# Keeping TensorE's source order in two stretches of a diffusion block's first mixer

## The chip, the cores and the metric

The kernel runs on one core of a Trainium2 chip. The metric is device time in microseconds (us), from launch to end, as a median of runs. The engines that matter here are TensorE (PE, matmuls and their weight loads), VectorE (DVE), ScalarE (ACT), GpSimd (POOL) and the queue of SyncE (SP), which issues most of the transfers. Each engine runs its own list of instructions in order; between engines they wait for each other through semaphores.

## The reference, cut to what matters

Two layers, each a mixer and a mixture of experts. The change touches the first mixer (`even_mixer`), which works on 256 context and 512 latent tokens, 768 in all:

```python
def even_mixer(a_lat, a_ctx, w_in, w_out, ...):
    cq_l, ckv_l, kr_l, rq_l, rk_l, rv_l, rg_l = split_cols(a_lat @ w_in, EVEN_SPLITS)
    ...                                   # the same for the context
    att_l = dense_block_attention(q_l, concat([k_c, k_l]), concat([v_c, v_l]))
    ret_l, ret_c = bidirectional_retention(...)
    y_lat = concat([att_l, retention_output(ret_l, rg_l, ret_norm_g)]) @ w_out

def modulation(cvec, w, b):               # six vectors of 1024 for each layer
    m = jax.nn.silu(cvec) @ w + b

def retention_output(o, g, gn_g):         # mean and variance over each head's 128 values
    y = head_layernorm(o, RET_GN_EPS).reshape(...) * gn_g
    return jax.nn.silu(g) * y
```

Attention has 8 heads of 64 + 32 (softmax over 256 keys for context rows and 768 for latent rows), retention has 4 heads of 128.

## The kernel before, in words

The program is written with a tile framework: pools hand out buffers in turn, semaphores come from the data, and a scheduler may reorder the instructions of each engine when the program is built. It lists them in the order in which they become ready in its own model of the machine. Inside `with tc.manual_schedule(engines={...PE})` the instructions of TensorE keep the order of the source; the other engines are still ordered by the scheduler. The experts' stage already runs inside such a block (L1695 to L2071), the first mixer does not.

The first mixer has two stretches that the change touches.

**Projections (L415 to L535).** `low_rank()` and `ret_proj()` are generators that make 20 column blocks of the input projection. Each block loads 128 columns of the weights (`load_w`: transfer `wraw`, then a high part by ACT, L401, and a low part by POOL, L402) and, after a `yield`, multiplies them with the activations in `proj_T`: for each half of the tokens (n = 0, 1) 8 row blocks k, and for each k three matmuls (L411 to L413), of `ah[k]`, `al[k]` and `ah[k]` again. `ah` and `al` are the high and low parts of the normalized activations, made just before by ACT (L380) and DVE (L382), one k after the other. At each `yield` two steps of the generator `ada` run: the modulation of both layers (`ada_gen`, L231), 40 chunks of 1 MB in all, each followed by 4 matmuls of 128x32 by 128x512 (8 records in the trace). Its ring holds 3 chunks, so the transfer of a chunk waits for the matmuls of the third before it.

**Attention beside retention (L556 to L704).** Two generators take turns, one step each. `mla()` runs 4 pairs of heads (hp) by 6 row tiles (t): `scores` (the matmuls `sc` into one of two double banks; row maximum L596 and its scaling L597 on DVE, exponential with row sum L599 on ACT, reciprocal L600 and multiplication of the row L601 on DVE, for head a = 0 and then a = 1, which I call P0 and P1 when done), a yield, then `values` of the tile before (matmuls `po`, L625) and `turn` of this one (transposes `ptp`, L615, of P0 and then P1, copied by ACT, L617). The step t = 0, 1 is narrow (256 keys: 2 `ptp` for a head, 4 `po`), t = 2 to 5 is wide (768 keys: 6 `ptp` for a head, 12 `po`); `values` belongs to the tile before, so the wide step t = 2 still has the 4 `po` of t = 1. Between t = 5 of a pair and its `turn` stands `heads` of the next pair (28 matmuls). `ret()` runs 4 heads by 6 tiles: the matmuls `rs` (L661, L671) and their masking on DVE (`sm`, L665, L674), a yield, then `rot` of the tile before (L694) and the matmuls `ro` (L682), whose statistics go through DVE (L686 to L688), a power on POOL (L689) and the normalization on DVE (`on`, L690). All banks other than those of `sc` come from one ring of four.

Because `heads` takes a step of its own, the two generators shift against each other by one step with each pair: for pairs 0 and 2 a step runs `sc`, `rot`, `ro`, `po`, `ptp`, `rs`; for pairs 1 and 3 it runs `rot`, `ro`, `sc`, `rs`, `po`, `ptp`.

Of the kernel before, what the change touches and what calls it, by code (L numbers as in the profile page):

```python
# [99 lines left out]
class Kern:  # L100
# [203 lines left out]
    def mixer0(self):  # L304
        nc, io, tc = self.nc, self.io, self.tc
# [24 lines left out]
        ada = self.ada_gen(0, 0)  # L330
# [53 lines left out]
        def ada_rest():  # L384
            for l, s in ((0, 1), (0, 2), (1, 0), (1, 1), (1, 2)):
                yield from self.ada_gen(l, s)
        ada = ada_rest()

        def load_w(cols, m=128):

            n = 32 if m == 64 else m
            raw = wsp.tile([128, 8, 128], F32, name="wraw")
            w = wsp.tile([128, 2, 8, 128], F32R, name="wblk")
            nc.sync.dma_start(raw[:, :, 0:n], wsrc[:, :, cols:cols + n])
            if m == 64:

                for b in range(2):
                    nc.vector.tensor_copy(
                        raw[:, :, 32:64].rearrange("p k (a b c) -> p k a b c", a=2, b=2)[:, :, :, b],
                        raw[:, :, 0:32].rearrange("p k (a b c) -> p k a b c", a=2, b=2)[:, :, :, 1 - b])  # L400
            nc.scalar.activation(w[:, 0, :, 0:m], raw[:, :, 0:m], AF.Copy)  # L401
            nc.gpsimd.tensor_tensor(w[:, 1, :, 0:m], raw[:, :, 0:m], w[:, 0, :, 0:m].bitcast(F32), OP.subtract)  # L402
            return w
# [21 lines left out]
        def low_rank():  # L425
            sqs = []
            for i in range(3):
                w = load_w(128 * i)
                dst = cqT[:, i] if i < 2 else ckvT
                sqt = new("sqt")  # L430
                sqs.append(sqt)

                def cb(n, t, p):
                    nc.scalar.activation(sqt[:, t], p, AF.Square)
                    nc.vector.tensor_copy(dst[:, t], p)
                yield
                proj_T(w, cb)
            nc.sync.dma_start(cs, io["k_cs"])
            nc.sync.dma_start(rcos, io["k_rcos"])
            nc.sync.dma_start(rsin, io["k_rsin"])  # L440
            w = load_w(384, 64)
            krt = new("krt")


            def cbk(n, t, p):
                nc.vector.tensor_tensor(krt[64:96, t], p[0:32], cs[64:96, t], OP.mult)
                nc.vector.tensor_tensor(kr[64:96, t], p[32:64], cs[96:128, t], OP.mult)
                nc.vector.tensor_tensor(kr[64:96, t], kr[64:96, t], krt[64:96, t], OP.add)
            yield
            proj_T(w, cbk, 64)  # L450
            nc.gpsimd.tensor_copy(kr[96:128], kr[64:96])
            for which in range(2):
                parts = sqs[0:2] if which == 0 else sqs[2:3]
                width = 256 if which == 0 else 128
                pbs = []
                for n in range(2):
                    pb = self.bank("ssb")
                    pbs.append(pb)
                    for i, s in enumerate(parts):
                        nc.tensor.matmul(pb[:, :384], self.ones, s[:, 384 * n:384 * n + 384], start=i == 0,  # L460
                                         stop=i == len(parts) - 1)
                rstd = new("rstd")
                for n, pb in enumerate(pbs):
                    r = rstd[:, 384 * n:384 * n + 384]
                    nc.vector.tensor_scalar(r, pb[:, :384], 1.0 / width, EPS, OP.mult, OP.add)
                    nc.scalar.activation(r, r, AF.Sqrt)
                    nc.vector.reciprocal(r, r)
                if which == 0:
                    for i in range(2):
                        nc.vector.scalar_tensor_tensor(cqT[:, i], cqT[:, i], self.qng[:, i:i + 1], rstd, OP.mult, OP.mult)  # L470
                else:
                    nc.vector.scalar_tensor_tensor(ckvT, ckvT, self.kvg, rstd, OP.mult, OP.mult)
# [54 lines left out]
        def ahead():  # L527
            yield from ret_proj()
            first.append(load(0))
        for gen in (low_rank(), ahead()):  # L530
            for _ in gen:
                next(ada, None)
                next(ada, None)
        for _ in ada:
            pass  # L535
        st_a.close()


# [111 lines left out]
        def ret():  # L650

            last = None
            for h in range(4):
                mk = bw.tile([128, 1536], F32, name="mk", bufs=1)
                nc.sync.dma_start(mk, io["k_masks"][h])
                for t in range(6):
                    ks_ = range(1, -1, -1) if t < 2 else range(5, 1, -1)
                    sm = bw.tile([128, 6, 128], F32, name="sm")
                    pb = self.bank("rs")
                    for i, kt in enumerate(ks_):  # L660
                        nc.tensor.matmul(pb[:, 128 * i:128 * i + 128], rk[h][:, 128 * kt:128 * kt + 128],  # L661
                                         rq[h][:, 128 * t:128 * t + 128], start=True, stop=True)
                    n = 128 * len(ks_)
                    m0 = 384 + 128 * (t - ks_[0])
                    nc.vector.tensor_tensor(sm[:, 0:len(ks_)], pb[:, 0:n].rearrange("p (k n) -> p k n", n=128),  # L665
                                            mk[:, m0:m0 + n].rearrange("p (k n) -> p k n", n=128), OP.mult)
                    order = list(ks_)
                    if t >= 2:
                        pb = self.bank("rs")
                        for i, kt in enumerate((1, 0)):  # L670
                            nc.tensor.matmul(pb[:, 128 * i:128 * i + 128], rk[h][:, 128 * kt:128 * kt + 128],  # L671
                                             rq[h][:, 128 * t:128 * t + 128], start=True, stop=True)
                        m0 = 896 + 128 * (t - 2)
                        nc.vector.tensor_tensor(sm[:, 4:6], pb[:, 0:256].rearrange("p (k n) -> p k n", n=128),  # L674
                                                mk[:, m0:m0 + 256].rearrange("p (k n) -> p k n", n=128), OP.mult)
                        order += [1, 0]
                    yield
                    if last:
                        last()
                    o = self.bank("ro")  # L680
                    for i, kt in enumerate(order):
                        nc.tensor.matmul(o[:, 0:128], sm[:, i], rv[:, kt, 128 * h:128 * h + 128], start=i == 0,  # L682
                                         stop=i == len(order) - 1)
                    stt = self.small.tile([128, 10], F32, name="stt", tag="stt")
                    on = bw.tile([128, 128], F32, name="on")
                    nc.vector.bn_stats(stt[:, 0:6], o[:, 0:128])  # L686
                    nc.vector.bn_aggr(stt[:, 6:8], stt[:, 0:6])
                    nc.vector.tensor_scalar(stt[:, 8:9], stt[:, 7:8], 1e-5, None, OP.add)  # L688
                    nc.gpsimd.tensor_tensor(stt[:, 9:10], stt[:, 8:9], self.mhalf[:, 0:1], OP.pow)  # L689
                    nc.vector.tensor_scalar(on, o[:, 0:128], stt[:, 6:7], stt[:, 9:10], OP.subtract, OP.mult)  # L690

                    def finish(h=h, t=t, on=on):
                        pt = self.bank("rot")
                        nc.tensor.transpose(pt[:, 0:128], on, self.ident)  # L694
                        s = slice(128 * t, 128 * t + 128)
                        nc.vector.scalar_tensor_tensor(retT[:, h, s], pt[:, 0:128], self.rgn[:, h:h + 1], rg[h][:, s],
                                                       OP.mult, OP.mult)
                    last = finish
                    yield
            last()  # L700

        gens = [mla(), ret()]
        while gens:
            gens = [g for g in gens if next(g, gens) is not gens]  # L704
        if "mix0" in self.dbg:
            nc.sync.dma_start(self.dbg["mix0"][:, 0:4], attT)
            nc.sync.dma_start(self.dbg["mix0"][:, 4:8], retT)
# [1444 lines left out]
```

## Time and profile before

| | |
|---|---|
| median of 3 runs | 2971.08 us (2970.87 to 2975.31) |
| profiled execution: time, span | 2972.21 us, 2970.4 us |
| TensorE busy in the span | 2660.2 us (90%) |
| VectorE, ScalarE, GpSimd busy | 1322.9, 742.6, 471.4 us |
| mean granted TensorE clock | 0.954 |

The first matmul of a projection starts 41.0 us into the span, the attention at 265.3, the output projection's last part ends near 555; the rest is the first expert stage, the second mixer (from about 1430) and the second expert stage. All times below are us from the start of the span. "Busy" of PE counts pipelined matmuls, so that two records can overlap.

### The profile page before, as it was taken

The page shows a single profiled execution, that of the slowest core. Times are in us where ns is not written, and L with a number is a line of the kernel's source. Part 1 is how long each engine was busy: PE and PEld are TensorE (multiplying, and loading weights), DVE is VectorE, ACT ScalarE, POOL GpSimd, SP SyncE. Part 2 cuts the span into 40 slices and gives each one's busy share as a digit, 9 for nine tenths or more (in the row PEclk, how much of TensorE's full clock was granted, in tenths as well). Part 3 has the DMA queues.
Part 4 walks back from the last instruction along what each step waited for, and adds up shares of the span by engine and source line. Part 5 has one row for each costly group of instructions (what it writes and reads, how often), then busy time and mean ns, then how long its engine had stood idle before and what let it go on. Part 6 is the DMA issues. An engine that isn't in the chain of part 4 may idle for free.

```text
span 2970.4 us, 47837 instructions
## 1 busy us (share of the span) xinstructions
PE 2660.2 (90%) x19606; PEld 1535.4 (52%) x19606; DVE 1322.9 (45%) x3546; ACT 742.6 (25%) x1718; POOL 471.4 (16%) x591
## 2 busy tenths in 40 slices
PE   7999999799999999999878878799987987888886
PEld 4787776544444444444466656587653332333322
DVE  4323665444234334322475777677654332223312
ACT  3212444211111111101354544366321111101111
POOL 2332003200000000000283553411210000000000
PEclk9999999799999999999987988899987999999999
DMA  9765001488988988988642233310349999999997
GB/s 329 244 246 175 27 12 57 172 333 353 371 356 355 371 345 367 365 355 355 216 126 73 86 108 120 111 32 28 118 184 377 426 427 427 427 426 427 426 427 314
DMA packets 176587, 779.47 MB, mean 262 GB/s; under 512 B 24327, under 2 KB 110768, under 8 KB 133488
## 3 DMA queue, kind: packets, MB, share of 16 engines
q1 hardware_dynamic: 169200, 752.31, 64.5%
q0 software_dynamic: 3872, 12.52, 1.2%
q10 hardware_dynamic: 3296, 11.58, 1.0%
q8 instruction: 155, 2.54, 0.4%
q14 instruction: 64, 0.52, 0.1%
HBM read 745.68 MB, written 30.67 MB: 261 GB/s over the span
## 4 chain that ended last, share of the span: by engine, by line
PE 64%; DMA 19%; DVE 9%; POOL 3%; ACT 3%; issue 2%; SPq 0%; POOLq 0%; ACTq 0%; DVEq 0%
PE gu L1924 13%; PE ydn L1992 9%; DMA wd<-in_moe_w_down_dram 8%; DMA we<-in_moe_w_gate_up_dram 8%; PE guc L1937 6%; PE ydc L1996 3%; PE pj L926 3%; PE pj L411 2%; PE pj L412 2%; PE pj L413 2%; PE op L774 2%; PE op L1556 2%; PE adap L231 2%; PE sc L593 1%; PE scp L1816 1%
## 5 line engine op out<-in xcount | busy, mean ns | idle before, releaser
L1924 PE MATMUL gu<-we,xs 128*64 128x512 f32 x3072 | 687.9, 597 | 83.5 <-DMA we<-in_moe_w_gate_up_dram 83.4
L1924 PEld LDWEIGHTS gu<-we,xs 128*64 128x64 f32 x3072 | 216.7, 137 | 520.5 <-issue 408.5
L1992 PE MATMUL ydn<-wd,uT 128*64 128x512 f32 x1536 | 351.8, 600 | 14.3 <-DMA wd<-in_moe_w_down_dram 13.7
L1930 DVE TENSOR_TENSOR sg<-gu,sg 64x512 f32<-64x512 f32 x96 | 66.5, 693 | 458.4 <-ACT sg L1929 457.8
L1929 ACT ACTIVATE sg<-gu 64x512 f32<-64x512 f32 x96 | 56.8, 592 | 846.3 <-PE gu L1924 846.3
L1776 POOL DMA_INDIRECT xg<-xnd,idx x22 | 20.9, 952 | 1246.6 <-DVE gate L1781 1186.0
L1992 PEld LDWEIGHTS ydn<-wd,uT 128*64 128x64 f32 x1536 | 107.9, 137 | 205.3 <-issue 187.0
L1937 PE MATMUL guc<-we,xs 128*32 128x256 f32 x3072 | 172.6, 380 | 0.0
L926 PE MATMUL pj<-aL,wblk 128*128 128x512 f32 x504 | 158.1, 448 | 0.0
L1937 PEld LDWEIGHTS guc<-we,xs 128*32 128x32 f32 x3072 | 96.4, 110 | 68.4 <-issue 7.5
L411 PE MATMUL pj<-ah,wblk 128*128 128x384 f32 (+1 forms) x320 | 109.5, 343 | 1.4 <-ACT ah L380 1.4
L926 PEld LDWEIGHTS pj<-aL,wblk 128*128 128x128 f32 x504 | 99.0, 210 | 18.4
L412 PE MATMUL pj<-al,wblk 128*128 128x384 f32 (+1 forms) x320 | 107.9, 338 | 0.0
L413 PE MATMUL pj<-ah,wblk 128*128 128x384 f32 (+1 forms) x320 | 107.4, 336 | 0.0
L1819 DVE TENSOR_TENSOR x<-scp,x 128x512 f32<-128x512 f32 x144 | 92.3, 684 | 30.3 <-PE scp L1817 29.4
L1996 PE MATMUL ydc<-wd,uTc 128*32 128x256 f32 x1536 | 90.6, 380 | 1.4 <-DMA wd<-in_moe_w_down_dram 1.4
L1906 DVE COPY uTc<-utc 128x128 f32<-128x128 f32 x48 | 14.0, 291 | 172.6 <-PE utc L1904 172.1
L2046 DVE TENSOR_TENSOR yp<-ydn,gbc 64x512 f32<-64x512 f32 x64 | 44.1, 689 | 103.8 <-PE ydn L1992 103.3
L1796 DVE TENSOR_SCALAR xs<-xst,gm,modT 128x128 f32<-128x128 f32 (+1 forms) x88 | 34.8, 397 | 118.9 <-PE xst L1788 115.7
L1900 ACT ACTIVATE uT<-utp 128x256 f32<-128x256 f32 x96 | 36.0, 375 | 159.4 <-PE utp L1899 158.6
L1382 DVE STREAM_TRANSPOSE Zbd<-X 64x256 f16<-64x256 f16 x144 | 62.7, 436 | 24.2 <-ACT X L1376 21.8
L1996 PEld LDWEIGHTS ydc<-wd,uTc 128*32 128x32 f32 x1536 | 47.6, 110 | 43.9 <-issue 15.2
(421 smaller groups left out, 4630.4 us busy)
## 6 DMA issues: line engine op xcount, KB each, us to landing
we<-in_moe_w_gate_up_dram SPq DMA_DIRECT2D x192, 2048.0 KB, 13.5
wd<-in_moe_w_down_dram SPq DMA_DIRECT2D x95, 2048.0 KB, 11.8
adaw<-in_ada_w_dram SPq DMA_DIRECT2D x48, 1024.0 KB, 6.5
wraw<-in_od_w_in_dram SPq DMA_DIRECT2D x33, 512.0 KB, 4.2
wraw<-in_ev_w_in_dram SPq DMA_DIRECT2D x19, 512.0 KB, 6.8
fb<-B SPq DMA_DIRECT2D x24, 256.0 KB, 2.5
BK<-fb SPq DMA_DIRECT2D x24, 256.0 KB, 3.0
xnd<-xn ACTq DMA_DIRECT2D x10, 512.0 KB, 4.7
```

Source lines behind the costliest of these rows:

```text
L231: nc.tensor.matmul(pb[32 * j:32 * j + 32], self.spad[:, k, :], w[:, 512 * j:512 * j + 512], start=k == 0, stop=k == 7, tile_position=(0, 3 ...
L411: nc.tensor.matmul(pb[:m, :384], w[:, 0, k, 0:m], ah[k][:, t], start=k == 0, stop=False)
L412: nc.tensor.matmul(pb[:m, :384], w[:, 0, k, 0:m], al[k][:, t], start=False, stop=False)
L413: nc.tensor.matmul(pb[:m, :384], w[:, 1, k, 0:m], ah[k][:, t], start=False, stop=k == 7)
L926: nc.tensor.matmul(pb[:, :n], w[:, i, k], a[j][:, k], start=k + i + j == 0, stop=k == 7 and i == 1)
L1382: nc.vector.transpose(Zd[h], X[hd[h]])
L1819: nc.vector.tensor_tensor(xs, pb, xs, OP.add)
L1924: nc.tensor.matmul(gu[64 * j:64 * j + 64, :], g.xs[:, k, 64 * a:64 * a + 64], ws[j][k], start=k == 0, stop=k == 7, tile_position=(0, 64 * j))
L1930: nc.vector.tensor_tensor(sg, gu[64:128], sg, OP.mult)
L1937: nc.tensor.matmul(guc[32 * j:32 * j + 32, 0:256], q.xs[:, k, 32 * a4:32 * a4 + 32], ws[j // 2][k][:, 256 * (j % 2):256 * (j % 2) + 256], ...
L1992: nc.tensor.matmul(y[64 * h:64 * h + 64, :], uT[:, f], wt[i][:, 512 * h:512 * h + 512], start=f == 0, stop=f == 11, tile_position=(0, 64 * h))
L1996: nc.tensor.matmul(yc[32 * j:32 * j + 32, 0:256], uTc[:, f], wt[i][:, 256 * j:256 * j + 256], start=f == 0, stop=f == 11, tile_position=(0 ...
```

## The change

The loop that drives the projections and the loop that drives attention and retention are each put into a `manual_schedule` block for TensorE. Nothing is computed otherwise, no buffer is added and no size changes.

```diff
-        for gen in (low_rank(), ahead()):
-            for _ in gen:
-                next(ada, None)
-                next(ada, None)
-        for _ in ada:
-            pass
+        with tc.manual_schedule(engines={mybir.EngineType.PE}):
+            for gen in (low_rank(), ahead()):
+                for _ in gen:
+                    next(ada, None)
+                    next(ada, None)
+            for _ in ada:
+                pass
         st_a.close()
...
-        gens = [mla(), ret()]
-        while gens:
-            gens = [g for g in gens if next(g, gens) is not gens]
+        with tc.manual_schedule(engines={mybir.EngineType.PE}):
+            gens = [mla(), ret()]
+            while gens:
+                gens = [g for g in gens if next(g, gens) is not gens]
```

What it moves in the lists of the engines stands at three places. Of the changed kernel the line numbers in the second stretch are two higher.

**TensorE, the first column block** (right after the activations' last transposes). Before:

```order
L231 MATMUL adap<-adaw,spad 32x512 x4
L411 MATMUL pj<-ah_395,wblk 128x384 x2
L412 MATMUL pj<-al_397,wblk 128x384
L413 MATMUL pj<-ah_395,wblk 128x384
L412 MATMUL pj<-al_397,wblk 128x384
L411 MATMUL pj<-ah_401,wblk 128x384
L413 MATMUL pj<-ah_395,wblk 128x384
L411 MATMUL pj<-ah_401,wblk 128x384
L231 MATMUL adap<-adaw,spad 32x512 x4
L412 MATMUL pj<-al_403,wblk 128x384
```

Of the change (`ah_395`, `ah_401`, `ah_407` are k = 0, 1, 2):

```order
L231 MATMUL adap<-adaw,spad 32x512 x8
L411 MATMUL pj<-ah_395,wblk 128x384
L412 MATMUL pj<-al_397,wblk 128x384
L413 MATMUL pj<-ah_395,wblk 128x384
L411 MATMUL pj<-ah_401,wblk 128x384
L412 MATMUL pj<-al_403,wblk 128x384
L413 MATMUL pj<-ah_401,wblk 128x384
L411 MATMUL pj<-ah_407,wblk 128x384
L412 MATMUL pj<-al_409,wblk 128x384
```

Before, both halves of the tokens advance together as `al[k]` comes in, with two more modulation chunks (8 matmuls) strewn among them; now the first half runs through all k, then the second, and the third and fourth chunk come after both. From the second column block on TensorE's list is the same in both kernels.

**TensorE, a wide step of pair 0** (`sc` first names head 0's keys, then head 1's). Before:

```order
L615 MATMUL ptp<-ks,P 128x128 x6
L593 MATMUL sc<-kT_2069,qT_2087 128x512
L615 MATMUL ptp<-ks,P 128x128 x6
L661 MATMUL rs<-rq_443,rk_447 128x128 x4
L671 MATMUL rs<-rq_443,rk_447 128x128 x2
L593 MATMUL sc<-kT_2069,qT_2087 128x256
L593 MATMUL sc<-kT_2070,qT_2096 128x512
L593 MATMUL sc<-kT_2070,qT_2096 128x256
L694 MATMUL rot<-ks,on 128x128
L682 MATMUL ro<-rv,sm 128x128 x6
L625 MATMUL po<-PT,V 64x128 x12
```

Of the change:

```order
L617 MATMUL ptp<-ks,P 128x128 x12
L663 MATMUL rs<-rq_443,rk_447 128x128 x4
L673 MATMUL rs<-rq_443,rk_447 128x128 x2
L595 MATMUL sc<-kT_2072,qT_2092 128x512
L595 MATMUL sc<-kT_2072,qT_2092 128x256
L595 MATMUL sc<-kT_2073,qT_2101 128x512
L595 MATMUL sc<-kT_2073,qT_2101 128x256
L696 MATMUL rot<-ks,on 128x128
L684 MATMUL ro<-rv,sm 128x128 x6
L627 MATMUL po<-PT,V 64x128 x12
```

The first score matmul of the next tile no longer stands between the transposes of head 0 and those of head 1. In the pairs 1 and 3 the same happens, there with one or two score matmuls.

**VectorE, the same step** (`nm_2396` and `nm_2406` belong to head 0 and 1, in the changed kernel `nm_2401` and `nm_2411`; `attT` is the copy of `po`). Before:

```order
L596 TENSOR_REDUCE nm_2406<-sc_2403 128x1
L696 SCALAR_TENSOR_TENSOR retT_2062<-rot_2413,vT_99,rg0_451 128x128
L600 RECIPROCAL nm_2396<-nm_2396 128x1
L597 TENSOR_SCALAR nm_2406<-nm_2406 128x1
L601 TENSOR_SCALAR P_2399<-P_2399,nm_2396 128x768
L686 BN_STATS stt_2423<-ro_2416 128x6
L687 BN_AGGR stt_2423<-stt_2423 128x2
L600 RECIPROCAL nm_2406<-nm_2406 128x1
L688 TENSOR_SCALAR stt_2423<-stt_2423 128x1
L601 TENSOR_SCALAR P_2409<-P_2409,nm_2406 128x768
L690 TENSOR_SCALAR on_2424<-ro_2416,stt_2423 128x128
L627 COPY attT_2061<-po_2430 128x128
```

Of the change:

```order
L598 TENSOR_REDUCE nm_2411<-sc_2408 128x1
L602 RECIPROCAL nm_2401<-nm_2401 128x1
L698 SCALAR_TENSOR_TENSOR retT_2065<-rot_2418,vT_99,rg0_451 128x128
L603 TENSOR_SCALAR P_2404<-P_2404,nm_2401 128x768
L599 TENSOR_SCALAR nm_2411<-nm_2411 128x1
L688 BN_STATS stt_2428<-ro_2421 128x6
L689 BN_AGGR stt_2428<-stt_2428 128x2
L690 TENSOR_SCALAR stt_2428<-stt_2428 128x1
L692 TENSOR_SCALAR on_2429<-ro_2421,stt_2428 128x128
L602 RECIPROCAL nm_2411<-nm_2411 128x1
L629 COPY attT_2064<-po_2435 128x128
L603 TENSOR_SCALAR P_2414<-P_2414,nm_2411 128x768
```

The scheduler orders VectorE anew around the fixed list of TensorE: the scaling of head 1's maximum, for which its exponential waits, now follows P0, and P1 now follows `on`, which waits for POOL. In the pairs 1 and 3 `on` stands ahead of head 0's maximum, where before part of that work came first.

## Rows read from the trace of the kernel before

**Rows 1.** Busy time by engine (instructions), clock, DMA; attention and retention.

```profile
265.30:473.60 208.30, 201.38 (x1459) 153.47 (x1459) 129.31 (x391) 85.07 (x201) 21.68 (x34) 0.98 0.19 61
```

**Rows 2.** Instructions in time: start, duration; PE in a wide step, pair 0.

```profile
300.73 0.87 PE L615 MATMUL ptp<-ks,P 128*128 128x128 f32 x6
...
307.56 1.53 PE L625 MATMUL po<-PT,V 128*64 128x128 f32 x24
...
309.02 0.87 PE L615 MATMUL ptp<-ks,P 128*128 128x128 f32 x6
...
309.73 1.02 PE L593 MATMUL sc<-kT,qT 128*128 128x512 f32 x2
...
310.60 0.82 PE L615 MATMUL ptp<-ks,P 128*128 128x128 f32 x6
```

**Rows 3.** Instructions in time: DVE, ACT and POOL in the same step.

```profile
306.22 0.96 DVE L596 TENSOR_REDUCE nm<-sc 128x1 f32<-128x768 f32 x1
307.01 0.19 ACT L599 ACTIVATION_READ_ACCUMULATOR P<-sc,nm 128x1 f32 x1
...
307.54 0.62 DVE L601 TENSOR_SCALAR P<-P,nm 128x768 f32<-128x768 f32 x1
...
307.65 0.90 ACT L599 ACTIVATE P<-sc,nm 128x768 f32<-128x768 f32 x1 [0.45 <-PE ro L682]
308.08 0.29 DVE L686 BATCH_NORM_STATS2 stt<-ro 128x6 f32<-128x128 f32 x1
...
308.88 0.62 DVE L601 TENSOR_SCALAR P<-P,nm 128x768 f32<-128x768 f32 x1
...
309.04 0.87 POOL L689 TENSOR_TENSOR stt<-stt,mhalf 128x1 f32<-128x1 f32 x1 [7.43 <-DVE stt L688]
...
309.94 0.41 DVE L690 TENSOR_SCALAR on<-ro,stt 128x128 f32<-128x128 f32 x1 [0.44 <-POOL stt L689]
310.27 0.28 DVE L627 COPY attT<-po 128x128 f32<-128x128 f32 x1
```

**Rows 4.** Instructions in time: a wide step of pair 1.

```profile
354.46 0.30 DVE L686 BATCH_NORM_STATS2 stt<-ro 128x6 f32<-128x128 f32 x1 [0.99 <-PE ro L682]
...
356.06 0.55 POOL L689 TENSOR_TENSOR stt<-stt,mhalf 128x1 f32<-128x1 f32 x1 [6.82 <-DVE nm L597]
...
358.49 0.61 DVE L601 TENSOR_SCALAR P<-P,nm 128x768 f32<-128x768 f32 x1
...
359.16 0.87 PE L615 MATMUL ptp<-ks,P 128*128 128x128 f32 x6 [0.21 <-DVE nm L597]
```

**Rows 5.** Instructions in time: PE, the first transposes of P.

```profile
281.02 1.31 PE L615 MATMUL ptp<-ks,P 128*128 128x128 f32 x4 [3.88 <-DVE nm L600]
```

**Rows 6.** Instructions in time: the first column block.

```profile
44.23 1.94 PE L231 MATMUL adap<-adaw,spad 128*32 128x512 f32 x8
...
52.55 0.96 DVE L382 TENSOR_TENSOR al<-aT,ah 128x768 fp32r<-128x768 f32 x1 [0.97 <-ACT ah L380]
...
54.01 1.07 PE L231 MATMUL adap<-adaw,spad 128*32 128x512 f32 x8
...
56.91 0.45 PE L411 MATMUL pj<-ah,wblk 128*128 128x384 f32 x1
...
58.06 0.33 PE L411 MATMUL pj<-ah,wblk 128*128 128x384 f32 x1
58.23 0.33 PE L412 MATMUL pj<-al,wblk 128*128 128x384 f32 x1
```

**Rows 7.** Instructions in time: two waits of PE in the second mixer.

```profile
1996.62 0.29 PE L1285 MATMUL pf<-X,Thbd 128*128 128x64 f16 x4 [1.53 <-DVE N L1452]
...
2065.95 0.29 PE L1285 MATMUL pf<-X,Thbd 128*128 128x64 f16 x4 [2.33 <-DVE N L1452]
```

**Rows 8.** Busy time by engine, then granted clock, around those two waits.

```profile
1995.00:2000.00 5.00, 3.47 (x55) 3.26 (x54) 4.04 (x15) 3.52 (x9) 0.54 (x2) 1.00 0.16 52
2065.00:2070.00 5.00, 4.02 (x25) 3.72 (x26) 3.89 (x13) 3.04 (x8) 0.40 (x1) 0.74 0.18 54
```

## The prediction, made before the changed kernel had run

> **What bounds the kernel now.** I first read busy time, waits and clock of the two stretches that the change touches. Attention beside retention is PE's: of 208.30 us PE is busy 201.38 at a granted clock of 0.98 [rows 1], so at most 6.9 us can be won there, and 3.88 of these are one wait ahead of the first transposes of P [rows 5]. Then I read one wide step in order of time. PE goes from `ptp` at 300.73 to `ptp` at 309.02, a step of 8.29 us, and none of its rows carries a wait [rows 2]. The other engines have slack only because of what PE does meanwhile: P0 ends at 307.54 + 0.62 = 308.16, P1 at 308.88 + 0.62 = 309.50, and `ptp` of head 1 is not wanted before 310.60, since a score matmul of the next tile fills 309.73 to 310.60 [rows 2, 3]. POOL's power and `on` come after P1, beside work that nobody waits for. Last I read the first column block: there PE follows DVE's `al[k]`, the last of which starts at 52.55 [rows 6].
>
> What comes after the mixer (routing, experts) hangs on its end, and the later lists of PE are alike in both kernels, so I carry a delay here to the end one to one.
>
> **The change, part by part: a wide step of pairs 0 and 2.** Nothing is added or removed; what counts is what PE finds ready. The score matmul of 310.60 - 309.73 = 0.87 leaves the gap between the heads, so PE wants P1 at 309.73. At the same time VectorE brings P1 later:
>
> - head 1's scaling now follows P0 (ends 308.16): about 308.05 + 0.14 (its row overlaps its predecessor by about 0.1), so the exponential starts near 308.3 instead of 307.65 and ends with its sum at 308.3 + 0.98 = 309.3 (0.90 and 0.19, overlapping) [rows 3].
> - `on` now stands ahead of P1. Statistics start near 308.1, as now; their three steps take 308.89 - 308.08 = 0.8, POOL's power starts 0.15 later, near 309.0. It took 0.87 in this step and 0.55 in the other kind [rows 3, 4]. With 0.55, `on` runs 309.55 to 309.95.
> - reciprocal, `attT` (0.28) and P1 (0.62) then end near 310.8; with about 0.06 to the next engine, `ptp` of head 1 starts at 310.86.
>
> PE waits 310.86 - 309.73 = 1.1 us, and the next `rs`, `sc` and everything behind it in its list wait too. That is the price of a full step: no engine makes it up, because the next P0 needs the next `sc`.
>
> I take 0.55 for the power, because P1's TENSOR_SCALAR (308.88 to 309.50) overlapped the long one (309.04), and will not any more; with 0.87 each of these steps costs 0.3 more, 6 x 0.3 = 2 us in all. The Trainium skill (SBUF — State Buffer, "Who interferes with whom") says that DVE and GpSimd share a pair of ports, which a tensor_scalar in its two-port form holds alone for the whole instruction. The two durations agree with that, and by that rule the sum stays as made, with 0.55.
>
> **A wide step of pairs 1 and 3.** Now: statistics at 354.46, power at 356.06 for 0.55, P0 at 358.49, `ptp` of head 0 at 359.16 after a wait of 0.21 [rows 4]. In the change `on` stands ahead of head 0's maximum. Statistics without the maximum between them end near 355.2, the power runs to 355.9, `on` (0.41) to 356.3; then the maximum (0.96) to 357.2, the scaling and the exponential to 358.45, while DVE does head 1's maximum and the first mask; P0 at 359.15 instead of 358.49. Scaling at 359.67, exponential of head 1 359.9 to 360.9, reciprocal, P1 361.15 to 361.8, `ptp` of head 1 at 361.83. PE without waits would have reached head 0's transposes at 359.16 - 0.21 = 358.95, plus 0.87 for the score matmul that now stands ahead of them, plus 0.71 (309.73 - 309.02) for the six transposes: 360.53. Wait: 1.3; I take 1.4, since P0 can add a little.
>
> **The sum over the stretch.** A wide step t = 2 has 4 `po` instead of 12. The step's 12 take 1.4 (307.56 to 309.02, 24 records), 4 a third of it, so PE is 0.9 earlier and waits that much more: 2.0 in pairs 0 and 2, 2.3 in pairs 1 and 3. Step t = 5 has the 28 matmuls of `heads` as cover, nothing. So: 4 full steps (t = 3, 4 of pairs 0 and 2) x 1.1 = 4.4; 3 full steps (t = 3, 4 of pair 1, t = 3 of pair 3) x 1.4 = 4.2; 4 steps t = 2, 2 x 2.0 + 2 x 2.3 = 8.6; t = 4 of pair 3, where `rs` has run out, 2.3. Wide: 19.5. Narrow steps: the first has its 3.88 already, and 0.9 of score matmul falls out of it: 0.9 [rows 5]. The other seven have short exponentials but only 4 `ptp`; no row shows them with a wait in the new order. From below nothing; from above the 1.7 that twice the missing 0.87 gives; I take 1.0, nearer to the wide steps: 7. Together 27.4. Some of the present 6.9 - 3.9 = 3.0 of small waits is absorbed by the new ones; I take off 2: **+25.5**. Bounds: if the order of DVE bites only by half in the wide steps and not in the narrow ones, 10 + 1 - 2 = +9; with 1.7 in the narrow ones and 0.87 for the power, 19.5 + 0.9 + 12 + 2 - 0 = +34.
>
> **The first column block.** Now both halves advance with `al[k]`, and the second block starts at 56.91 [rows 6]. In the change half 0 has to wait for the last `al`, 52.55 + 0.96 = 53.5, and is done near 54.1. Only then half 1 runs: 24 matmuls at 0.173 each (58.06 to 58.23) = 4.2, then the two chunks strewn in so far, 2 x 1.07 = 2.1. The second block starts at 60.4 instead of 56.91, +3.5. While PE follows DVE with half of its matmuls it idles more than now, so the clock can be at its lower level when half 1 begins (1.2 instead of 2.4 GHz, so twice the spacing): from above 24 x 0.35 = 8.3, +7.6. I take **+5**. The modulation's transfers stay ahead: their chunks are used later than now, not earlier, except for chunk 1.
>
> **Sum** on the profiled execution's own 2972.2 (1.1 above the median): 2972.2 + 25.5 + 5 = 3002.7, so 3003.
>
> **The clock** stands apart, as it can change most. In dense work a PE gap of 1.53 left the granted clock at 1.00; one of 2.33 went with a clock of 0.74 in its 5 us [rows 7, 8]. My waits of 1.1 to 1.4 lie under the first, those of 2.0 to 2.3 between the two. I count none. A clock of 0.74 over 5 us is 5 x 0.26 = 1.3 us of PE's work lost, and as much again if it lasts another 5 us: a fall costs 1.3 to 2.6, say 2. The Trainium skill (TensorE: Matmul & The Clock Gate, "A second HAM failure mode: psum-queue depth-cycling") says that frequent short idles between groups of matmuls make the clock swing, with throughput lost at each return. By the page's rule the clock would swing in this stretch; the gap of 1.53 here speaks against it, the one of 2.33 for it.
>
> **The rivals.**
> 1. *The clock falls in the wide steps.* For it: 2.33 against 0.74. Against it: 1.53 against 1.00. A loss of 2 in each of 13 wide steps (12 with a wait, and the first narrow one) adds 26: 3029, 3015 to 3040.
> 2. *The waits are hidden.* `on` and the scaling come up to 1 us earlier than I place them, or P1 is not late because the whole of VectorE moves up behind an earlier `rs`. Then the 0.87 of score matmul merely changes places and only the first block costs: 2977, 2973 to 2985. For it: DVE is busy only 153.47 of 208.30 [rows 1]. Against it: the step is a chain from `sc` to P1, and not DVE's load sets it.
> 3. *Faster.* Chunk 1 of the modulation is now used before the first block instead of at 44.23 [rows 6], which frees a buffer of the ring about 4.5 us earlier. If the projections waited for modulation transfers, all later chunks would come up to 5 us sooner: 2967. It decides only where PE waits for these transfers; what PE waits for in the first block is DVE and, behind it, ACT, as the row of the last `al` shows, no transfer, so I give it little.
>
> **How the numbers follow.** Forecast (VectorE's new order lays P1 bare in most steps) 0.72, with its own range of 2985 to 3013, from 2972.2 + 9 + 3.5 to 2972.2 + 34 + 7.6 rounded down. Clock 0.13, hidden 0.12, faster 0.03. The range 2985 to 3030 leaves out the hidden case, the faster one and the upper part of the clock case (0.12 + 0.03 + about 0.05), 2 in 10. About 6 us, 0.2%, is what a measurement of this kernel can tell from no change; of the hidden case three parts in four lie within that: faster 0.03, same 0.09, slower 0.88.
>
> **What would show it.** In the changed profile PE waits ahead of the second half of `ptp` (now L617) in each wide step, released by DVE P at L603, about 1.1 in pairs 0 and 2, 1.4 in pairs 1 and 3, 2 or more at t = 2; the stretch from the first attention matmul to the last grows from 208 to about 234 with busy time unchanged; the second column block starts at 60 to 63; POOL's power lasts 0.55 in all steps; the clock stays at 0.95 or more in the stretch. I am wrong if those waits are under 0.4, if a granted clock near 0.8 stands in the stretch, or if the output projection ends as late as now while something behind it is late.

## The result, and the profile after

The changed kernel takes 2999.02 us (median of 4 runs, 2998.18 to 3006.05), against 2972.43 us for the kernel before on the same chip: a ratio on record of 1.0094, with a 95% interval of 1.0076 to 1.0111 (the two medians alone give 1.0089). Forecast were 3003 us, range 2985 to 3030. The profiled execution's span went from 2970.4 to 2997.4 us, +27.0.

Reading both traces by places of the program splits the 27.0:

| from the start of the span, us | before | after | difference |
|---|---|---|---|
| attention's first matmul | 265.30 | 271.77 | +6.5 |
| from there to the output projection's first matmul | 200.39 | 223.75 | +23.4 |
| output projection, first to last | 88.25 | 85.53 | -2.7 |
| from there to the experts' first matmul | 33.75 | 32.91 | -0.8 |
| the experts' first matmul stands at | 587.69 | 613.96 | +26.3 |

The rest of the program is 0.7 us longer. So the loss has two places, the first column block and attention, and it is kept to the end but for 3.5 us.

The grouped instructions of TensorE in attention say what the longer stretch consists of (mean ns of one, then the idle time ahead of the group with its releasers). The transposes of P, before:

```profile
L615 PE MATMUL ptp<-ks,P 128*128 128x128 f32 x212 | 32.0, 282 | 4.9 <-DVE nm L600 3.9 <-DVE P L601 0.5 <-DVE nm L597 0.2
```

And after:

```profile
L617 PE MATMUL ptp<-ks,P 128*128 128x128 f32 x212 | 33.0, 289 | 26.0 <-DVE P L603 17.2 <-DVE nm L602 4.8 <-DVE nm L599 2.7
```

The same 212 records wait 26.0 us instead of 4.9, and 17.2 of them for the multiplication of P. Busy time of the engines and granted clock in the stretch, before and after (the columns, as in [rows 1]: stretch, length, then busy time and records of PE, of PE's weight loads, of VectorE, ScalarE and GpSimd, then clock, DMA share, GB/s):

```profile
265.30:465.69 200.39, 193.47 (x1413) 148.84 (x1413) 127.92 (x388) 82.80 (x196) 21.68 (x34) 0.98 0.17 55
```

```profile
271.77:495.52 223.75, 197.54 (x1412) 152.41 (x1412) 130.03 (x387) 82.67 (x196) 19.29 (x34) 0.97 0.16 51
```

PE's idle time grew from 6.9 to 26.2 us, 19.3 of the 23.4; PE's busy time grew by 4.1 with one record fewer, at a clock of 0.97; the part on why the prediction was right estimates that most of these 4.1 are two falls of the clock. VectorE and ScalarE do nearly the same work (127.9 and 130.0 us, 82.8 and 82.7).

A wide step of pair 0 after the change, in order of time, answers to [rows 2, 3]:

```profile
318.10 0.15 DVE L599 TENSOR_SCALAR nm<-nm 128x1 f32<-128x1 f32 x1
318.33 0.90 ACT L601 ACTIVATE P<-sc,nm 128x768 f32<-128x768 f32 x1 [1.13 <-DVE nm L599]
...
319.00 0.55 POOL L691 TENSOR_TENSOR stt<-stt,mhalf 128x1 f32<-128x1 f32 x1 [8.86 <-DVE stt L690]
319.07 0.88 PE L617 MATMUL ptp<-ks,P 128*128 128x128 f32 x6
...
319.58 0.41 DVE L692 TENSOR_SCALAR on<-ro,stt 128x128 f32<-128x128 f32 x1 [0.73 <-POOL stt L691]
...
320.17 0.61 DVE L603 TENSOR_SCALAR P<-P,nm 128x768 f32<-128x768 f32 x1
320.83 0.88 PE L617 MATMUL ptp<-ks,P 128*128 128x128 f32 x6 [0.89 <-DVE P L603]
```

VectorE stands idle for 0.73 in front of `on`, because POOL's power ends at 319.55. P1 ends at 320.78, and PE, through with head 0 at 319.94, has waited 0.89. The step of pair 1 answers to [rows 4]:

```profile
371.58 0.41 DVE L692 TENSOR_SCALAR on<-ro,stt 128x128 f32<-128x128 f32 x1 [0.73 <-POOL stt L691]
371.91 0.95 DVE L598 TENSOR_REDUCE nm<-sc 128x1 f32<-128x768 f32 x1
...
376.82 0.62 DVE L603 TENSOR_SCALAR P<-P,nm 128x768 f32<-128x768 f32 x1
377.59 0.85 PE L617 MATMUL ptp<-ks,P 128*128 128x128 f32 x6 [1.22 <-DVE P L603]
```

Here head 0's maximum waits for `on`, everything of both heads follows late, and PE waits 1.22. The first column block answers to [rows 6]:

```profile
41.49 1.67 PE L231 MATMUL adap<-adaw,spad 128*32 128x512 f32 x8 [1.44 <-DMA adaw<-in_ada_w_dram]
...
51.84 0.52 PE L412 MATMUL pj<-al,wblk 128*128 128x384 f32 x1 [2.71 <-DVE al L382]
...
54.08 0.96 DVE L382 TENSOR_TENSOR al<-aT,ah 128x768 fp32r<-128x768 f32 x1 [0.97 <-ACT ah L380]
...
55.09 0.69 PE L412 MATMUL pj<-al,wblk 128*128 128x384 f32 x1 [0.30 <-DVE al L382]
...
61.53 1.92 PE L231 MATMUL adap<-adaw,spad 128*32 128x512 f32 x16
63.38 0.44 PE L411 MATMUL pj<-ah,wblk 128*128 128x384 f32 x1
```

The second block starts at 63.38 instead of 56.91. But the last `al` itself starts at 54.08 instead of 52.55 [rows 6], so 1.5 of the 6.5 us come ahead of it; e10 returns to this. Granted clock over this part, in stretches of 5 us, was 0.64, 0.71 and 0.61 from 45 to 60, where it had been 0.83, 1.00 and 1.00:

```profile
45.00:50.00 5.00, 3.92 (x12) 3.54 (x12) 5.00 (x5) 2.82 (x4) 2.82 (x1) 0.64 1.09 377
50.00:55.00 5.00, 2.57 (x6) 1.45 (x6) 4.03 (x7) 1.69 (x2) 0.00 (x0) 0.71 0.70 275
55.00:60.00 5.00, 4.91 (x18) 4.91 (x19) 0.60 (x2) 0.49 (x1) 0.00 (x0) 0.61 0.00 0
```

### The profile page after: what moved, and what is told of

Same layout as the page of the kernel before. It is cut to its first block, busy times and chain, and to the rows that moved or that the text cites. A ratio compares the mean times of both kernels' runs of the same rounds, so it can differ in the third digit from the quotient of the medians.

```text
span 2997.4 us, 47845 instructions
## 1 busy us (share of the span) xinstructions
PE 2674.5 (89%) x19606; PEld 1546.9 (52%) x19606; DVE 1321.7 (44%) x3546; ACT 741.5 (25%) x1718; POOL 467.2 (16%) x591
## 4 chain that ended last, share of the span: by engine, by line
PE 51%; DMA 17%; DVE 8%; ACT 3%; POOL 3%; issue 2%; SPq 0%; POOLq 0%; ACTq 0%; DVEq 0%
PE gu L1928 14%; PE ydn L1996 9%; DMA we<-in_moe_w_gate_up_dram 8%; DMA wd<-in_moe_w_down_dram 7%; PE guc L1941 6%; PE ydc L2000 3%; PE pj L930 3%; PE op L778 2%; PE op L1560 2%; PE scp L1820 1%; PE pe L1402 1%; PE scp L1821 1%; PE utp L1903 1%; PE sw L1204 1%; DVE Thbd L1342 1%
## 5 line engine op out<-in xcount | busy, mean ns | idle before, releaser
L1386 DVE STREAM_TRANSPOSE Zbd<-X 64x256 f16<-64x256 f16 x144 | 62.7, 436 | 24.2 <-ACT X L1380 22.0
## 6 DMA issues: line engine op xcount, KB each, us to landing
we<-in_moe_w_gate_up_dram SPq DMA_DIRECT2D x192, 2048.0 KB, 13.6
```

The lines of the kernel that those rows point to most:

```text
L1386: nc.vector.transpose(Zd[h], X[hd[h]])
```

## The experiments

The theory: VectorE's new order (`on`, which waits for POOL, ahead of P1 or of the maximum) makes P1 late just where the score matmul that covered it has gone. The rivals: the missing score matmul alone, whatever VectorE does; the late scaling rather than `on`; the clock. For the first block: the order of the halves, against the early chunk.

One table for all runs; "starts" is attention's first matmul, "attention" from there to the output projection's first, "ptp idle" the idle time ahead of all transposes of P in it, "experts" the first matmul of the experts. Each ratio is against runs of the kernel before in the same job. Some matmuls of attention still run beside the output projection's first: the last ends 6.2 to 6.5 us behind that mark in e3, e4, e5, e7 and e9 and 7.9 behind it in all others, so against the others "attention" of these five is up to 1.7 too long.

| run | starts | attention | ptp idle | experts | median, us | ratio, 95% interval |
|---|---|---|---|---|---|---|
| before | 265.30 | 200.39 | 4.9 | 587.69 | 2972.43 | |
| changed | 271.77 | 223.75 | 26.0 | 613.96 | 2999.02 | 1.0094 (1.0076 to 1.0111) |
| e1 projections only | 270.73 | 199.50 | 4.6 | 592.01 | 2974.36 | 1.0015 (1.0004 to 1.0025) |
| e2 attention only | 265.38 | 224.56 | 26.7 | 609.23 | 2992.49 | 1.0062 (1.0040 to 1.0085) |
| e3 score between | 269.74 | 206.88 | 13.6 | 594.77 | 2979.95 | 1.0026 (1.0014 to 1.0037) |
| e4 vector order | 269.69 | 218.57 | 14.5 | 605.62 | 2990.54 | 1.0066 (1.0048 to 1.0085) |
| e5 `on` before P1 | 270.19 | 227.73 | 28.2 | 618.16 | 3004.01 | 1.0108 (1.0076 to 1.0140) |
| e6 first block | 265.70 | 198.96 | 4.2 | 586.79 | 2970.52 | 1.0001 (0.9985 to 1.0018) |
| e7 score between, vector order | 270.86 | 212.39 | 11.4 | 600.24 | 2986.70 | 1.0047 (1.0032 to 1.0062) |
| e8 gate late | 265.10 | 196.72 | 1.8 | 584.07 | 2969.12 | 0.9989 (0.9973 to 1.0004) |
| e9 score between, `on` before P1 | 270.18 | 214.93 | 19.9 | 604.11 | 2987.89 | 1.0064 (1.0041 to 1.0086) |
| e10 second chunk late | 269.39 | 200.38 | 4.6 | 591.91 | 2976.32 | 1.0027 (1.0015 to 1.0039) |
| e11 first block, gate late | 265.71 | 196.54 | 2.4 | 582.63 | 2966.88 | 0.9992 (0.9982 to 1.0003) |

**e1 and e2: each half of the change alone.** The other loop is put back as before (shown for e1).

```diff
-        with tc.manual_schedule(engines={mybir.EngineType.PE}):
-            gens = [mla(), ret()]
-            while gens:
-                gens = [g for g in gens if next(g, gens) is not gens]
+        gens = [mla(), ret()]
+        while gens:
+            gens = [g for g in gens if next(g, gens) is not gens]
```

> The changed kernel with the scheduler back in attention beside retention; only the projections keep TensorE's source order. Theory (two separate costs): the first column block's loss alone, about 6.5 us as its profile shows (second block's first matmul at 63.4 instead of 56.9), so 2978 to 2980, with no waits ahead of the transposes of P beyond those of before. Rival (the loss in the first block is made up later, because the modulation's transfers run ahead): 2972, and then all 26 us belong to attention.

> The changed kernel with the scheduler back in the projections; only attention beside retention keeps TensorE's source order. Theory: 20 us more than before, 2991 to 2994, with the waits ahead of ptp as in the changed kernel (0.8 to 0.9 in pairs 0 and 2, 1.2 in pairs 1 and 3). Rival (part of the loss in attention comes from the later start, for example from transfers that now collide): fewer or shorter waits, 2980 to 2988.

e1 starts attention 5.4 us late, is as fast as before within it, and reaches the experts 4.3 late; its median is 3.0 above, less than the 2978 to 2980 expected, but the interval of its ratio is 1.2 to 7.4 us (0.0004 and 0.0025 of 2971). e2 starts attention on time and loses 24.2 in it, 21.5 by the experts' first matmul, its waits being those of the changed kernel (26.7 ahead of `ptp`). The two costs are separate; the late start does not make the waits.

**e3: the score matmul put back between the heads, by hand.**

```diff
                 for a in range(2):
+                    if a == 1 and 1 <= t < 5:
+                        s = self.bank2("sc")
+                        nc.tensor.matmul(s[:, 0:512], qT[0][:, 128 * t + 128:128 * t + 256],
+                                         kTs[2 * hp % 4][:, 0:512], start=True, stop=True)
+                        pre.append(s)
```

> The changed kernel, with the source of attention rewritten so that the first score matmul of the next tile is issued between the transposes of head 0 and head 1 (inside one pair of heads). TensorE still keeps source order; VectorE's list, which the scheduler makes, then has the scaling of head 1's maximum ahead of P0 and `on` behind P1 again. Theory (missing cover, and the order of VectorE that follows from it): the waits ahead of the second ptp fall under 0.3, attention takes 208 to 212 us and the whole 2978 to 2982. Rival (keeping source order costs by something else, such as the clock or the banks of the ring): 2990 or more.

Attention falls from 223.75 to 206.88, a little below the 208 to 212 of the theory, and the whole to 2979.95, as the theory had it. In the list of VectorE that the scheduler made for this kernel, `on` stands behind P1 again in pairs 0 and 2, and their wide waits are gone. In pairs 1 and 3 there is a remainder, above the 0.3 expected: the head whose P comes first waits at t = 2, and P1 costs 0.35 in a full step instead of 1.22:

```profile
349.43 0.88 PE L625 MATMUL ptp<-ks,P 128*128 128x128 f32 x6 [1.09 <-DVE nm L600]
...
360.64 0.85 PE L625 MATMUL ptp<-ks,P 128*128 128x128 f32 x6 [0.35 <-DVE P L604]
```

**e4: TensorE's list of the changed kernel, VectorE in an order of its own.** Two things change at once in e3, so e4 changes VectorE alone: both scalings early, then the reciprocal and the multiplication (`normalize`) of P0 and P1, and `on` last, just ahead of the masks of the next `rs`.

```diff
+                    Ps.append((P, nm))
+                for a in range(2):
+                    normalize(*Ps[a])
...
-                    nc.vector.tensor_scalar(on, o[:, 0:128], stt[:, 6:7], stt[:, 9:10], OP.subtract, OP.mult)
+                    def norm(on=on, o=o, stt=stt):
+                        nc.vector.tensor_scalar(on, o[:, 0:128], stt[:, 6:7], stt[:, 9:10], OP.subtract, OP.mult)
+                    late.append(norm)
...
-        with tc.manual_schedule(engines={mybir.EngineType.PE}):
+        with tc.manual_schedule(engines={mybir.EngineType.PE, mybir.EngineType.DVE}):
```

> The changed kernel with TensorE's list as it is, but VectorE also keeps source order in attention, and that source is written so that both heads' maxima and scalings come first, then P0 and P1, and `on` behind them. Theory (VectorE's order lays P1 bare): the wait ahead of head 1's ptp goes to at most 0.2 in pairs 0 and 2 and under 0.6 in pairs 1 and 3; 2983 to 2987. Rival (it is the missing score matmul alone: PE is simply 0.87 us too early whatever VectorE does): waits of 0.8 and more stay, 2996 to 3000.

P1 is hardly what PE waits for any more: of 17.2 us only 1.9 are left. But attention falls by 5.2 us alone, to 218.57, 18.2 above before, and the expected 2983 to 2987 were missed (so was the rival's 2996 to 3000), since other waits come out from under it. By groups, with the transposes now on line 621:

```profile
L621 PE MATMUL ptp<-ks,P 128*128 128x128 f32 x212 | 33.6, 288 | 14.5 <-DVE on L701 6.6 <-ACT PT L623 3.8 <-DVE P L609 1.9
```

In order of time, one of pair 0 and one of pair 1:

```profile
314.67 0.55 PE L621 MATMUL ptp<-ks,P 128*128 128x128 f32 x3 [0.37 <-ACT PT L623]
```

```profile
359.67 1.84 PE L621 MATMUL ptp<-ks,P 128*128 128x128 f32 x12 [0.70 <-DVE on L701]
```

The transposes take their banks from the ring of four: in pairs 0 and 2 one still holds transposes that ACT is copying, in pairs 1 and 3 one holds `ro`, which is free when `on` has read it. As long as P1 came later than these banks, neither wait showed. That is read from the releasers and the source; no run gave the ring another bank.

**e5: the same with `on` ahead of P1 again.** Of VectorE's two moves this leaves only that of `on` (with the statistics, which it needs, P1 stands behind it).

```diff
                    yield
+                    normalize(*Ps[1])
                     if last:
                         values(*last)
                     PT = turn(t, Ps)
```

> As the run with both engines in source order, with TensorE's list of the changed kernel, but VectorE has `on` ahead of P1 again and head 1's reciprocal and P1 just ahead of `attT`; both scalings stay early. It splits the two changes in VectorE's order. Theory A (`on`, which waits for POOL, is what makes P1 late; the scaling of head 1 behind P0 hides under that wait): waits of 0.6 to 0.9 on P1 in pairs 0 and 2 and 0.9 to 1.3 in pairs 1 and 3, attention 220 to 223 us. Theory B (the late scaling, and so the late exponential, is the cause): waits of 0.2 or less in pairs 0 and 2, attention 216 to 219 us.

Theory A holds: with both scalings early the waits of pairs 0 and 2 are 0.92 to 0.99 in the full steps, and 28.0 of 28.2 us are P's:

```profile
L620 PE MATMUL ptp<-ks,P 128*128 128x128 f32 x212 | 33.6, 288 | 28.2 <-DVE P L608 28.0
```

Its sizes were off: pairs 1 and 3 wait less (0.49 in a full step at head 1), the narrow steps more than in the changed kernel (0.85 to 1.71, and 1.38 and 3.64 in the first), and attention is 227.73 where 220 to 223 was expected. What the late scaling costs when `on` is not in front of it, no run shows.

**e7 and e9: the two other corners.** Both have the score matmul between the heads as e3, with the order of VectorE of e4 (e7) and of e5 (e9). Their edits are those of e3 and of e4 or e5 together.

> The changed kernel with both rewrites of attention: the first score matmul of the next tile between the heads, and VectorE in the source order with P0 and P1 early and `on` late. Theory (the score matmul covers PE's wait for P1 as well as that for the banks that ACT and `on` free): no wait over 0.3 in the wide steps, attention 199 to 203 us from its first matmul to the output projection's first, the whole 2972 to 2976 with the first block's loss. Rival (the banks behind `on` and the copies of ptp set the pace with the score matmul too): waits of 0.4 to 0.7 stay, attention 206 or more.

> The run that has `on` ahead of P1, with the first score matmul of the next tile between the heads added: the fourth corner of score matmul (without, with) by `on` (ahead of P1, behind it). Theory (P1 late and cover gone are both needed: the 0.87 us of score matmul covers a wait of 0.9): waits of 0.1 in the wide steps of pairs 0 and 2, none in pairs 1 and 3, the narrow waits stay (0.8 to 1.7); attention 208 to 214 us. Rival (the price of `on` ahead of P1 is paid whatever PE does in between): waits of 0.5 and more in pairs 0 and 2, 220 us or more.

| attention, us | without the score matmul | with it | worth |
|---|---|---|---|
| `on` ahead of P1 | 227.73 (e5) | 214.93 (e9) | 12.8 |
| `on` behind P1 | 218.57 (e4) | 212.39 (e7) | 6.2 |
| the scheduler's own order | 223.75 (changed) | 206.88 (e3) | 16.9 |

The score matmul is worth twice as much where `on` makes P1 late, and `on` costs 9.2 us without it and 2.5 with it: each covers part of the other, so neither theory alone is enough. In pairs 0 and 2 it comes out as expected in the full steps: no wait of 0.35 or more at t = 3 and 4 in e7 nor in e9; at t = 2 waits of 0.75 (e7) and of 0.96 and 1.03 (e9) stay. In pairs 1 and 3 e7's rival was right, for a late `on` there holds back the bank of the next transposes, with the score matmul behind them:

```profile
359.32 1.04 PE L629 MATMUL ptp<-ks,P 128*128 128x128 f32 x6 [0.70 <-DVE on L709]
```

This suggests that `on` belongs behind P1 in pairs 0 and 2 and ahead of the transposes in pairs 1 and 3; neither of the two places tried is right for both, and a source with a place for each was not run. e9 kept waits of 0.41 in the full steps of pairs 1 and 3 and of 1.27 at t = 2, where none was expected. The best of the six is still the scheduler's own order with the score matmul back (e3).

**e6: the first column block with k outside and the halves inside.**

```diff
+            pbs = [self.bank("pj") for n in range(2)]
+            for k in range(8):
+                for n in range(2):
+                    t = slice(384 * n, 384 * n + 384)
+                    nc.tensor.matmul(pbs[n][:, :384], w[:, 0, k], ah[k][:, t], start=k == 0, stop=False)
+                    nc.tensor.matmul(pbs[n][:, :384], w[:, 0, k], al[k][:, t], start=False, stop=False)
+                    nc.tensor.matmul(pbs[n][:, :384], w[:, 1, k], ah[k][:, t], start=False, stop=k == 7)
+                if k == 3:
+                    next(ada, None)
```

> The changed kernel with the scheduler back in attention, and with the source of the first column block rewritten: k outside, the two halves of the tokens inside (two banks), one modulation chunk ahead of the block, one after k = 3. Theory (the loss of the first block is the order of its halves and the early chunk): attention starts at 265 to 266.5 instead of 270.7 and the whole is that of before, 2970 to 2973. Rival (source order costs in the blocks behind it too): attention at 268 or later.

Attention starts at 265.70 and the median does not differ from before: source order costs nothing that shows in the other 19 blocks.

**e10: of the first block's two edits, the early chunk alone taken back.**

```diff
                 for _ in gen:
                     next(ada, None)
-                    next(ada, None)
+                    if ada1:
+                        next(ada, None)
+                    if len(ada1) == 1:
+                        next(ada, None)
+                    ada1.append(0)
```

> As the run with source order in the projections alone, but the second modulation chunk of the first step comes behind the first column block instead of ahead of it; the order of the halves stays. Theory (the loss is the order of the halves; the early chunk's wait for its transfer hides in PE's wait for the last al): attention starts at 270.5 to 272, no earlier than with the chunk ahead. Rival (the early chunk's wait of 1.4 us is part of the loss): attention starts at 268.5 to 269.5.

Attention starts at 269.39, 1.3 before e1, while the seven profiles with unchanged source-order projections lie between 269.69 and 271.77. That is as far as the rival wanted it, but the median is no lower than e1's, and most of the 1.3 is not the chunk. The last `al` itself starts 0.84 earlier; it depends on work ahead of the early chunk, and its start differs from run to run. e1, then e10:

```profile
53.38 0.96 DVE L382 TENSOR_TENSOR al<-aT,ah 128x768 fp32r<-128x768 f32 x1 [0.97 <-ACT ah L380]
```

```profile
52.54 0.96 DVE L382 TENSOR_TENSOR al<-aT,ah 128x768 fp32r<-128x768 f32 x1 [0.97 <-ACT ah L380]
```

Counted from this start, attention begins 217.2 to 217.7 us later in those seven profiles, 216.9 in e10, and 212.2 to 212.8 in the five with the block of before or of e6. So the block costs 4.5 to 5.5 us. Of these the early chunk may be 0.4 to 0.9; the rest, 4.1 to 4.6, is the order of the halves together with the chunks that came to stand behind the block, both of which e6 took back at once.

**e8 and e11: is there a faster version?** The 3.88 us of [rows 5] stood in the kernel before too. e8 is the kernel before with the gate's additions on POOL made late (`after` is a column of `retT` of the third tile), e11 is e6 with the same.

```diff
         brow = pool.tile([128, 1024], F32, name=f"brow{s}", tag="brow")
+        if after is not None:
+            nc.gpsimd.tensor_copy(brow[:, 0:1], after)
```

> The kernel before, with one more thing: the transfer of the gate's bias row waits for a column of retT written in the third tile (a copy of one column by POOL), so that POOL's two large additions of the gate rows no longer stand ahead of the first powers. Theory (the 3.88 us wait ahead of the first transposes of P, and the fall of the clock there, come from these additions): that wait falls under 1.5, no 5 us at half clock near 281, 2964 to 2968. Rival (the additions only move and stop a later power by as much): 2970 to 2973.

> The two changes that lost nothing together: first column block in source order with the halves inside k, scheduler in attention, and the gate's additions late. Theory: attention starts at 265 to 266.5 and takes 196 to 198 us; if what is won there reaches the end, 2966 to 2969, 3 to 4 us under the kernel before. Rival (the experts' stages behind give it back): 2970 to 2972.

In e8 the wait at the first transposes of P is 0.59 instead of 3.88:

```profile
277.53 0.41 PE L617 MATMUL ptp<-ks,P 128*128 128x128 f32 x2 [0.59 <-DVE nm L602]
```

The clock, 0.88 and 0.50 from 275 to 285 before, is 0.83 and 0.83. Attention is 3.7 us shorter, and the experts start 3.6 earlier (e11: 3.9 and 5.1). The additions on POOL were the cause of that wait. The medians are 2.0 and 3.0 us lower, but both intervals reach over 1: no gain is proven at the end. e8's 2969.12 lies between the ranges of its theory and its rival, e11's 2966.88 in that of its theory.

## Why the prediction was right

*One list fixed, another remade.* The waits came where the forecast put them, ahead of head 1's `ptp` and released by P. That VectorE's remade order makes P1 late was right: e4 takes 15.3 of P1's 17.2 us away with TensorE's list unchanged. That `on` behind POOL is enough for it was right (e5). But this order is the smaller part of the loss. Mending it alone gave back 5.2 us of attention (e4), putting the score matmul back gave 16.9 (e3), and no run has an order of VectorE with which the changed list of TensorE loses nothing. The forecast's full step has both terms, the 0.87 of cover gone and the late P1; what it did not have are the banks, which stand close behind P1.

*The size in the wide steps.* Forecast and measured waits: full steps of pairs 0 and 2 1.1 and 0.83 to 0.90; of pairs 1 and 3 1.4 and 1.22; t = 2 of pairs 0 and 2 2.0 and 1.68 to 1.75; of pairs 1 and 3 2.3 and 0.88 + 1.21, which is 2.1; the last 2.3 and 0.99 + 1.06. Wide together 19.5 and 16.8. POOL's power lasted 0.55 in 23 of 24 steps (0.67 in the other), as taken. That agrees with what the Trainium skill (SBUF — State Buffer, "Who interferes with whom") says of the port pair: in the step shown above VectorE runs nothing while the power runs.

*The narrow steps* were the mis-sized term: 7 us forecast for the seven after the first, and four waits of 0.72 to 0.94 measured with four small ones of 0.16 to 0.28, 4.0 in all. The first grew from 3.88 to 4.84, by 0.96 where 0.9 was forecast. 16.8 + 4.8 + 4.0 = 25.6 of the 26.0 us in the row of `ptp`.

*The sum* of attention, put at 25.5 (27.4 less 2 is 25.4), is 23.4 measured. That it came so near is in part luck: PE's idle time grew by 19.3, 6 less than forecast, and PE's busy time, which the forecast left unchanged, added 4.1.

*The first block*, +5 forecast with bounds of 3.5 and 7.6, costs 4.9 us in this profile and 4.5 to 5.5 over the seven, counted from the last `al`; the other 1.5 of the 6.5 came before it. The working holds too: half 1 runs only behind the last `al`, from 55.90 to 61.53, which is 5.6 us instead of 4.2, its first ten matmuls 0.32 apart at the lower clock and the rest 0.17. The forecast's "no transfer" was wrong in one place: chunk 1, placed ahead of the block, waits 1.44 for its transfer. As PE still waits 2.71 and 0.30 for `al` after that, little of it can count, and e10 bounds it.

*One to one to the end* held for all but the 3.5 us that output projection and routing gave back. Of these, 1.1 is PE's wait for `acut` inside the output projection (the rest I could not assign), 2.78 before:

```profile
490.04 9.60 PE L774 MATMUL op<-w,acut 128*128 128x512 f32 x34 [2.78 <-DVE acut L766]
```

and 1.64 after:

```profile
518.73 6.65 PE L778 MATMUL op<-w,acut 128*128 128x512 f32 x28 [1.64 <-DVE acut L770]
```

*The rivals.* The hidden case fell with the waits above, the faster one with the late second block. For the hidden case the forecast named VectorE's busy time as 153.47; that column of [rows 1] is PE's weight loads, VectorE's is the next, 129.31. No term of the sum hangs on it.

*The clock*, for which the forecast counted nothing, did fall, though in two places and not in each wide step. Over the stretch it is 0.97. Besides the fall at the first transposes of P (0.50 in 5 us before and after) there is one near 415 and one near 490:

```profile
410.00:415.00 5.00, 3.18 (x26) 2.76 (x25) 2.22 (x9) 2.63 (x6) 0.55 (x1) 0.89 0.01 3
415.00:420.00 5.00, 5.00 (x22) 3.61 (x21) 2.62 (x5) 0.44 (x1) 0.00 (x0) 0.77 0.01 3
...
485.00:490.00 5.00, 2.95 (x33) 2.50 (x30) 2.81 (x8) 2.75 (x6) 0.00 (x0) 0.90 0.42 120
490.00:495.00 5.00, 5.00 (x29) 3.10 (x29) 1.94 (x3) 1.75 (x4) 0.00 (x0) 0.76 0.57 195
```

An estimate from these rows: (0.11 + 0.23) x 5 us and (0.10 + 0.24) x 5 us are 1.7 us each at most, and 1.5 each if only PE's busy time is counted. Together that is 3.0 to 3.4, most of the 4.1 by which PE's busy time grew. The forecast's price of a fall, 1.3 to 2.6, was right, its count of none was not.

## What to carry to other kernels

Fixing one engine's order in a scheduled program remakes the lists of the others: read those too, and look for an instruction that waits for a slow third engine and now stands ahead of one that TensorE needs. A matmul of the next tile between two dependent groups is worth what is late behind it, here 6 to 17 us by the order of VectorE. A wait that is taken away uncovers the next one below it (here, banks still being read), so price a repair by the second longest wait too. Before a start that comes late is put down to the change, look whether what it waits for came late ahead of the change.

## What the runs showed of the hardware

The same wait was followed by a lower clock in one run and not in another. In the changed kernel PE waited 1.75 us at pair 2's t = 2, and the clock of the 5 us behind it was 0.77 (row above); in e2, with the same wait at the same place, it stayed at 1.00. The wait in the changed kernel, then wait and clock (third column from the end) in e2:

```profile
413.16 0.85 PE L617 MATMUL ptp<-ks,P 128*128 128x128 f32 x6 [1.75 <-DVE P L603]
```

```profile
407.53 0.85 PE L615 MATMUL ptp<-ks,P 128*128 128x128 f32 x6 [1.75 <-DVE P L601]
```

```profile
410.00:415.00 5.00, 5.00 (x45) 3.98 (x43) 3.94 (x11) 1.58 (x3) 0.00 (x0) 1.00 0.02 3
```

In e2 the clock fell at other places instead, to 0.80 in the 5 us from 460 and to 0.82 in those from 485. The second fall of the changed kernel came with waits of 0.99 and 1.06, and in e7 even a wait of 3.59 left the clock at 1.00:

```profile
476.05 0.30 PE L714 MATMUL rot<-ks,on 128*128 128x128 f32 x1 [3.59 <-DVE on L709]
```

```profile
475.00:480.00 5.00, 3.95 (x40) 3.16 (x41) 1.55 (x4) 0.87 (x2) 0.00 (x0) 1.00 0.41 115
```

The length of a wait alone did not decide it, and the forecast's bounds of 1.53 and 2.33 [rows 7, 8] were no threshold. The rule of the Trainium skill that short idles make the clock swing (TensorE: Matmul & The Clock Gate, "A second HAM failure mode: psum-queue depth-cycling") is borne out in part: with 19 waits of 0.7 to 1.8 us in the stretch the clock fell twice more than before, and was 0.97 against 0.98.
